# Moving four kinds of transposes of a hybrid decoder block onto one PSUM bank of their own, out of a rotation of four

## The chip, the cores and the metric

The kernel runs on one core of a Trainium2 chip. The metric is the device time of one execution in microseconds, as the median of several runs. Of the kernel before there are three runs, 2709.86, 2710.72 and 2713.3 us, with a median of 2710.72 us.

## What is computed

One layer of a decoder block on 2048 tokens of width 1024, in float32:

```python
h = modulate(rms_norm(x, g_pre), shift, scale)      # adaLN from the conditioning vector c
z = h @ W_in    # attention q|k|v, mLSTM q|k|v|o, mLSTM i|f gates, branch gates A|B
y_A = sliding_window_attention(rope(q), rope(k), v, sinks)   # 8 query heads, 2 kv heads of 64, window 128
y_B = mlstm(conv4_silu(q), conv4_silu(k), v, i, f)           # 4 heads of 128, per-head norm, output gate
x = x + gate * rms_norm((sigmoid(g_A) * (y_A @ W_A) + sigmoid(g_B) * (y_B @ W_B)) @ W_out)
x = x + gate2 * rms_norm(swiglu(modulate(rms_norm(x, .), shift2, scale2)))   # width 2816
```

## The kernel before, in words

**Staging.** The 2048 tokens are done in two superblocks of 1024, sb0 and sb1, each made of two groups b0 and b1 of 512 tokens (four tiles t0 to t3 of 128 rows). A superblock first makes h for b1 (`hprep`, with `one()` at L515 that transposes h, and `hsums` at L552), then the projections of b0 and b1 in the order q and k|v|gates of b0 (`q_kv`), attention in the background, mLSTM values of b0 (`vm`), k|v of b1, q of b1, mLSTM values of b1. Then come the larger projections as a seven-product Strassen-like scheme (`pair_parts`), with the mLSTM chunks in the background, and the output projections. After both superblocks the SwiGLU layer (gate and up, then down) runs, in the same scheme, from about 1250 us on.

**Arithmetic.** A float32 operand is split into a rounded fp32r high part and a low part (`whi` and `wlo` of weights, by ScalarE at L259 and VectorE at L260; `hl` of the pairs at L1356 and L1357), and each product is three matmuls, high·high, high·low, low·high. Scores and the value products of attention run on half of TensorE's rows or columns for each of the two kv heads g0 and g1, so that two matmuls of different heads can lie beside one another.

**PSUM.** There are eight banks. Four carry the tag `acc` (the projections' accumulators) and four the tag `mix`, for all else: the transposes of h (L515), of queries (`q_stream`, L767), of keys (`k_stream`, L794), of the gates (`gates`, L846 and L877), the four score banks of an attention block (L921), its transposed probabilities (L954) and its value products (L966), and in the mLSTM the transposed keys `pk` (L1015), the state updates `pcn` (L1032), the scores `pS` (L1048), the outputs `pn` (L1059) and their transposes `py` (L1086). Later `mix` also holds the FFN's half of the banks (L1398, L1590, L1756).

```python
def mix_tile():
    return ps_mix.tile([P, 512], F32, tag="mix", name=nm("mix"))
```

A pool gives out the banks of one tag in the order in which the program asks for them. The n-th `mix` tile can be written when the (n−4)-th has been read for the last time. On TensorE the first writes of `mix` tiles stand in rising order of their number.

**What sets the order.** The program text interleaves generators by an estimate of elapsed time (`now[0]`); a background stream (a query tile's rotation and transpose, a key tile's, an attention block, an mLSTM chunk) is taken up when its due time has come. What the text asks for first has the smaller tile number. Then, at build time, a scheduler simulates the program with the dependences of its tiles and buffers, and orders the instructions of each engine by it. Each engine then runs its instructions in that fixed order, and waits where an input or a buffer isn't there.

**Other buffers that the steps touch.** The tag `tx` has 9 buffers: an evacuated q tile takes two (`raw` and the rotation's `z`, then the high and low part at L771 and L772, which are written to DRAM as `at_d`), a k|v tile two, an mLSTM value tile one. They come free when the transposes and the DMA out have ended. The probabilities and the mLSTM operands take the tag `tm` (9 buffers). An attention block loads its queries, keys and values from `at_d` into `at`, scores them, makes the softmax (copies L931 and L933, exponentials L946, scaling by GpSimd L950), transposes the probabilities, multiplies by the values (L966) and stores. Two streams of attention blocks run side by side.

Of the kernel before, what the change touches and what calls it, by code (L numbers as in the profile page):

```python
# [19 lines left out]
P = 128  # L20
# [51 lines left out]
def decoder_block(ctx: ExitStack, tc: tile.TileContext, a: dict, out: bass.AP, dbg=None):  # L72
# [24 lines left out]
    def acc_tile():  # L97
        return ps_acc.tile([P, 512], F32, tag="acc", name=nm("acc"))

    def mix_tile():  # L100
        return ps_mix.tile([P, 512], F32, tag="mix", name=nm("mix"))

    def tx(shape, dtype=F32):
        return tpool.tile(shape, dtype, tag="tx", name=nm("tx"), bufs=9)
# [631 lines left out]
    def superblock(sb):  # L736
# [27 lines left out]
        def q_stream(b, t, yz):  # L764
            yield L_ROPE
            y, z = yz
            pt = mix_tile()  # L767
            for j in range(GQ):
                transpose(pt[:, j * P:(j + 1) * P], y[:, j * P:(j + 1) * P])
            hi, lo = z.bitcast(F32R), y.bitcast(F32R)  # L770
            A.activation(hi, pt, AF.Copy, scale=HD ** -0.5)  # L771
            V.scalar_tensor_tensor(lo, pt, HD ** -0.5, hi.bitcast(F32), op0=ALU.mult, op1=ALU.subtract)  # L772
            for i, q in enumerate((hi, lo)):
                nc.sync.dma_start(at_d[b * NT + t][:, i * 512:(i + 1) * 512], q.bitcast(F32))
# [16 lines left out]
        def k_stream(n, yz):  # L791
            yield L_ROPEK
            y, z = yz
            pt = mix_tile()  # L794
            transpose(pt[:, :P], y)
            kk = z[:, P:3 * P].bitcast(F32R).rearrange("p (i k) -> p i k", i=2)
            A.copy(kk[:, 0, :], pt[:, :P])
            V.tensor_tensor(kk[:, 1, :], pt[:, :P], kk[:, 0, :].bitcast(F32), op=ALU.subtract)
            for n_, u in ((n, 1), (n + 1, 0)):
                if n_ < S // P:  # L800
                    nc.sync.dma_start(at_d[n_][:, AT_K:AT_V].rearrange("p (i u k) -> p i u k", i=2, u=2)[:, :, u, :], kk.bitcast(F32))
# [199 lines left out]
        def chunk_state(c):  # L1001
            b, t = b0 + c // NT, c % NT
            negm_d, mp, cl, ex = R["gates", b]
            cs = slice(t * P, (t + 1) * P)
            n_ = b * NT + t
            Cnew = c_tile(n_ + 1)
            km, qm = ld([MH, P]), ld([MH, P])
            nc.sync.dma_start(km, qk_d[b][:, 1, :, cs])
            nb = tm([P, MH, P])
            nc.sync.dma_start(nb, negm_d[:, cs].unsqueeze(0).to_broadcast([P, MH, P]))  # L1010
            nc.sync.dma_start(qm, qk_d[b][:, 0, :, cs])
            vc = vmt[n_ % 2]
            nc.sync.dma_start(vc[:, :, :MD], vm_d[b][:, t, :].rearrange("p (h d) -> p h d", h=MH))
            yield L_LOAD
            pk = mix_tile()  # L1015
            for hh in range(MH):
                transpose(pk[:, hh * P:(hh + 1) * P], km[:, hh, :])
            kw = tm([P, MH, P])
            V.tensor_tensor(kw, pk.rearrange("p (h d) -> p h d", h=MH), ex[:, 0, t, :].unsqueeze(2).to_broadcast([P, MH, P]), op=ALU.mult)
            wd = tm([P, MH, P])  # L1020
            V.tensor_tensor(wd, nb, cneg.unsqueeze(1).to_broadcast([P, MH, P]), op=ALU.add)
            for hh in range(MH):
                A.activation(wd[:, hh, :], wd[:, hh, :], AF.Exp, bias=cl[:, t, 0, hh:hh + 1])
            qs_ = None
            if n_ > 0:
                qs_ = tm([P, MH, P])
                G.tensor_tensor(qs_, nb, mp[:, :, t].unsqueeze(2).to_broadcast([P, MH, P]), op=ALU.add)
                A.activation(qs_, qs_, AF.Exp)
                G.tensor_tensor(qs_, qs_, qm, op=ALU.mult)
            R["w", c] = wd, qs_, km, qm, vc  # L1030
            yield L_KW
            pcn = [mix_tile() for _ in range(2)]  # L1032
            for hh in range(MH):
                mm(pcn[hh // 2][:, (hh % 2) * 129:(hh % 2) * 129 + 129], kw[:, hh, :], vc[:, hh, :], True, True)
            for hh in range(MH):
                o = pcn[hh // 2][:, (hh % 2) * 129:(hh % 2) * 129 + 129]
                if n_ == 0:
                    V.tensor_copy(Cnew[:, hh, :], o)
                else:
                    V.scalar_tensor_tensor(Cnew[:, hh, :], C[n_][:, hh, :], ex[:, 2, t, hh:hh + 1], o, op0=ALU.mult, op1=ALU.add)  # L1040

        def chunk_out(c):
            b, t = b0 + c // NT, c % NT
            negm_d, mp, cl, ex = R["gates", b]
            cs = slice(t * P, (t + 1) * P)
            n_ = b * NT + t
            wd, qs_, km, qm, vc = R["w", c]
            pS = mix_tile()  # L1048
            for hh in range(MH):
                mm(pS[:, hh * P:(hh + 1) * P], km[:, hh, :], qm[:, hh, :], True, True)  # L1050
            V.tensor_tensor(wd, pS.rearrange("p (h t) -> p h t", h=MH), wd, op=ALU.mult)
            yield L_S
            om = tm([P, MH, P])
            nc.sync.dma_start(om, om_d[b][:, :, cs])
            den = small.tile([P, MH], F32, tag="den", name=nm("den"))
            st = small.tile([P, MH, 6], F32, tag="st", name=nm("st"))
            mv = small.tile([P, MH, 2], F32, tag="mv", name=nm("mv"))
            vr = small.tile([P, MH], F32, tag="vr", name=nm("vr"))
            pn = [mix_tile() for _ in range(2)]  # L1059
            for hh in range(MH):  # L1060
                o = pn[hh // 2][:, (hh % 2) * 129:(hh % 2) * 129 + 129]
                if n_ > 0:
                    mm(o, qs_[:, hh, :], C[n_][:, hh, :], True, False)
                mm(o, wd[:, hh, :], vc[:, hh, :], n_ == 0, True)
            for hh in range(MH):
                V.bn_stats(st[:, hh, :], pn[hh // 2][:, (hh % 2) * 129:(hh % 2) * 129 + P])
            for h2 in range(2):
                V.tensor_copy(den[:, 2 * h2:2 * h2 + 2], pn[h2][:, :258].rearrange("p (u w) -> p u w", u=2)[:, :, P])
            for hh in range(MH):
                V.bn_aggr(mv[:, hh, :], st[:, hh, :])  # L1070
            V.scalar_tensor_tensor(den, den, -1.0, den, op0=ALU.mult, op1=ALU.max)
            V.tensor_tensor(den, den, ex[:, 1, t, :], op=ALU.max)
            V.reciprocal(den, den)
            V.tensor_tensor(vr, mv[:, :, 1], den, op=ALU.mult)
            V.tensor_tensor(vr, vr, den, op=ALU.mult)
            V.tensor_scalar(vr, vr, EPS, None, op0=ALU.add)
            cf = small.tile([P, MH], F32, tag="cf", name=nm("cf"))
            G.tensor_tensor(cf, vr, nhalf[:, :MH], op=ALU.pow)
            V.tensor_tensor(cf, cf, den, op=ALU.mult)
            V.scalar_tensor_tensor(vr, mv[:, :, 0], -1.0, cf, op0=ALU.mult, op1=ALU.mult)  # L1080
            ym = tm([P, MH, P])
            for hh in range(MH):
                o = pn[hh // 2][:, (hh % 2) * 129:(hh % 2) * 129 + P]
                A.activation(ym[:, hh, :], o, AF.Identity, scale=cf[:, hh:hh + 1], bias=vr[:, hh:hh + 1])
            yield L_LN
            py = mix_tile()  # L1086
            for hh in range(MH):
                transpose(py[:, hh * P:(hh + 1) * P], ym[:, hh, :])
            V.tensor_tensor(om, py.rearrange("p (h t) -> p h t", h=MH), om, op=ALU.mult)
            yh, yl = tm([P, MH, P], F32R), tm([P, MH, P], F32R)  # L1090
            A.copy(yh, om)
            V.tensor_tensor(yl, om, yh.bitcast(F32), op=ALU.subtract)
            for i, y in enumerate((yh, yl)):
                nc.sync.dma_start(y_d[b][:, 2 + i, :, cs], y.bitcast(F32))
# [283 lines left out]
    def h_combine(b2, rows, quarters, sums):  # L1378
# [14 lines left out]
        for k in range(4):  # L1393
            xk = xn
            v = {}
            for j, (half, i) in enumerate(QUADS):
                kk = k + 4 * half
                ps = mix_tile()  # L1398
                for t in range(4):
                    transpose(ps[:, t * P:(t + 1) * P], xk[j][:, t, :])  # L1400
                q = quarters()
# [64 lines left out]
    def pair_parts(w, c0, done, new, spare, bank):  # L1466
# [4 lines left out]
        def make(i, prep):  # L1471
            B = PROD[i][1]

            def mms(wt):
# [11 lines left out]
                    mm(ps, l[1], r[0], False, kk == 3, True)  # L1486
                    yield
                combine(i, ps, R, new, done)
            return Part(raw, prep, mms, weave=bank is not mix_tile, ahead=4)

        for i, prep in enumerate(a_operands(raw, spare)):
            yield make(i, prep)
# [67 lines left out]
    def gate_up(b2):  # L1560
        late = None
        for p in range(NP):
# [24 lines left out]
                for n, t_ in (("S1", s1_), ("S3", a_["21"]), ("S2", s2_), ("S4", s4_)):  # L1587
                    nc.sync.dma_start(as_d[b2][:, IDX[n], p, :], t_)

            gp, up = (list(pair_parts(w, p * 256, done, unit, unit, mix_tile)) for w, done in ((wg, done_g), (wu, done_u)))  # L1590
            load, sums = down_weights(p)
            if F.get("late") is not None and p == 0:
                def a_step():
# [33 lines left out]
    def down(b2):  # L1627
# [105 lines left out]
        def make(raw, i, p, j):  # L1733
# [16 lines left out]
            def mms(ab):  # L1750
                if p == 0:
                    for t in range(NT):
                        if i == 0:
                            R[t]["X"] = acc_tile()
                        if i not in IN_X:
                            R[t]["Y"] = mix_tile()  # L1756
                if hold:
                    F.setdefault("held", []).append((p, ab))
                    if p == NP - 1:
# [110 lines left out]
```

## Time and profile before

| | |
|---|---|
| median of 3 runs | 2710.72 us (2709.86 to 2713.3) |
| profiled execution, its own time | 2716.59 us |
| its span on the core | 2714.9 us |
| TensorE matmul busy | 2639.2 us, 97% of the span |
| VectorE busy | 1986.2 us, 73% |
| ScalarE busy | 1299.8 us, 48% |
| GpSimd busy | 148.2 us, 5% |

The profiled execution took 5.87 us more than the median. Of TensorE's 75.7 us that aren't busy, 23.5 lie in the first 50 us and 9.1 after 2700 us. In the rows of the trace PE is TensorE, DVE is VectorE, ACT ScalarE, POOL GpSimd. A timeline row gives the start, the time from the start of the first to the end of the last instruction of a group, the engine, line and tiles, and in brackets the idle time before it and who ended it. One value product in float32 is one row of the program and two instructions of the trace.

### The profile page before, as it was taken

To read this page: it belongs to the slowest core of one execution; us is meant where nothing else is said; L and a number is where in the kernel's file an instruction comes from. 1 tells how busy PE (TensorE), PEld (TensorE's weight loads), DVE (VectorE), ACT (ScalarE), POOL (GpSimd) and SP (SyncE) were. 2 spreads that over 40 slices of the span, in tenths; PEclk is the share of its full clock that TensorE was granted. 3 is DMA by queue.
4 is the path that set the end of the run, shared out by engine and by line. 5 is a ranking of instruction groups with operands and counts; after the bars stand their busy time and mean duration, and the time that the engine had idled before them with its cause. 6 is when DMAs were issued, how large, how long until landed. Compare 5 with 4: busy or idle time off the path is not lost.

```text
span 2714.9 us, 35793 instructions
## 1 busy us (share of the span) xinstructions
PE 2639.2 (97%) x12310; PEld 2138.9 (79%) x12310; DVE 1986.2 (73%) x3906; ACT 1299.8 (48%) x2558; POOL 148.2 (5%) x189
## 2 busy tenths in 40 slices
PE   6989999999998999999999999999999999999998
PEld 4867788888885678888887888888877888888886
DVE  7968788778695778876687777776677676766456
ACT  5556544444755564444563443335554333333444
POOL 2010001100101000110000000000000000000000
PEclk8999999999998999999999999999999999999999
DMA  7654355897574544678765564436675232324566
GB/s 249 206 184 157 128 172 179 269 340 248 196 235 147 196 138 138 213 231 291 251 224 198 175 201 152 155 113 213 215 271 188 97 117 86 113 97 144 186 210 217
DMA packets 353639, 511.90 MB, mean 189 GB/s; under 512 B 25120, under 2 KB 213660, under 8 KB 348208
## 3 DMA queue, kind: packets, MB, share of 16 engines
q1 hardware_dynamic: 353456, 509.61, 56.9%
q8 instruction: 97, 1.59, 0.2%
q14 instruction: 86, 0.70, 0.1%
HBM read 357.12 MB, written 144.02 MB: 185 GB/s over the span
## 4 chain that ended last, share of the span: by engine, by line
PE 85%; DVE 7%; DMA 4%; ACT 2%; issue 1%; POOL 0%; SPq 0%; DVEq 0%; ACTq 0%; POOLq 0%
PE acc L204 61%; PE mix L204 22%; PE mix L209 2%; DVE hl L1357 1%; DVE tm L428 1%; DMA raw<-as_d 1%; ACT tm L946 1%; ACT hl L1356 1%; DMA raw<-in_w_in_dram 1%; DMA at_d<-tx 0%; DMA big<-in_x_dram 0%; DVE wlo L260 0%; DMA tx<-in_w_ada_dram 0%; DVE w L1667 0%; DMA at<-at_d 0%
## 5 line engine op out<-in xcount | busy, mean ns | idle before, releaser
L204 PE MATMUL acc<-big,hl 128*128 128x512 f32 x3936 | 940.8, 394 | 4.3 <-ACT tx L827 1.8
L204 PEld LDWEIGHTS acc<-big,hl 128*128 128x128 f32 x3936 | 733.3, 188 | 172.5 <-issue 13.8
L1356 ACT CAST hl<-raw 128x512 fp32r<-128x512 f32 x732 | 440.1, 621 | 493.4 <-PE acc L204 222.2
L1357 DVE TENSOR_TENSOR hl<-raw,hl 128x512 fp32r<-128x512 f32 x732 | 496.3, 694 | 194.8 <-ACT hl L1356 194.0
L204 PE MATMUL acc<-whi,big 128*128 128x512 f32 (+1 forms) x1280 | 379.3, 377 | 10.8 <-ACT big L518 8.4
L204 PEld LDWEIGHTS acc<-whi,big 128*128 128x128 f32 x1280 | 236.2, 192 | 52.4 <-ACT big L518 8.5
L204 PE MATMUL mix<-big,hl 128*128 128x512 f32 x1056 | 263.9, 391 | 1.7 <-ACT hl L1356 1.1
L204 PE MATMUL acc<-wlo,big 128*128 128x512 f32 (+1 forms) x640 | 241.2, 379 | 6.4 <-DVE wlo L260 6.4
L204 PE MATMUL acc<-hl,hl 128*128 128x512 f32 x1008 | 237.4, 393 | 5.1 <-DVE hl L1357 3.4
L204 PEld LDWEIGHTS mix<-big,hl 128*128 128x128 f32 x1056 | 197.9, 188 | 45.9 <-ACT hl L1356 1.9
L204 PEld LDWEIGHTS acc<-hl,hl 128*128 128x128 f32 x1008 | 187.0, 188 | 50.9 <-DVE hl L1357 8.8
L204 PE MATMUL mix<-hl,hl 128*128 128x512 f32 x792 | 182.7, 391 | 1.3 <-DVE hl L1357 0.9
L204 PEld LDWEIGHTS mix<-hl,hl 128*128 128x128 f32 x792 | 147.9, 188 | 35.3 <-DVE hl L1357 3.1
L204 PE MATMUL acc<-big,whi 128*128 128x512 f32 x512 | 157.4, 393 | 0.0
L260 DVE TENSOR_TENSOR wlo<-raw,whi 128x1024 fp32r<-128x1024 f32 (+1 forms) x96 | 109.0, 1137 | 65.5 <-ACT whi L259 59.8
L259 ACT CAST whi<-raw 128x1024 fp32r<-128x1024 f32 (+1 forms) x96 | 94.3, 983 | 123.8 <-PE acc L204 110.4
L204 PEld LDWEIGHTS acc<-wlo,big 128*128 128x128 f32 x640 | 123.7, 193 | 28.3 <-DVE wlo L260 8.6
L475 POOL TENSOR_TENSOR rs<-ms,nhalf 128x1 f32<-128x1 f32 (+1 forms) x56 | 42.6, 772 | 1617.5 <-DVE ms L473 1610.5
L204 PE MATMUL mix<-hcT4h,hl 128*128 128x512 f32 x352 | 117.7, 395 | 0.7 <-ACT hl L1356 0.7
L204 PE MATMUL acc<-hcT2h,hl 128*128 128x512 f32 x352 | 117.6, 394 | 0.0
L204 PEld LDWEIGHTS acc<-big,whi 128*128 128x128 f32 x512 | 95.4, 188 | 19.2
L204 PE MATMUL acc<-big,wlo 128*128 128x512 f32 x256 | 97.7, 393 | 0.0
(330 smaller groups left out, 3491.5 us busy)
## 6 DMA issues: line engine op xcount, KB each, us to landing
raw<-in_w_in_dram SPq DMA_DIRECT2D x48, 1024.0 KB
as_d<-w SPq DMA_DIRECT2D x154, 256.0 KB
raw<-as_d SPq DMA_DIRECT2D x70, 512.0 KB
raw<-in_w_ffn_gate_dram SPq DMA_DIRECT2D x22, 1024.0 KB
raw<-in_w_ffn_up_dram SPq DMA_DIRECT2D x22, 1024.0 KB
raw<-ws_d SPq DMA_DIRECT2D x40, 512.0 KB
y_d<-tm SPq DMA_DIRECT2D x64, 256.0 KB
tx<-in_w_ada_dram SPq DMA_DIRECT2D x64, 256.0 KB
```

The costliest lines, as they stand in the source:

```text
L204: T.matmul(o, lhsT=lhsT, rhs=rhs, start=start, stop=stop, skip_group_check=resumed)
L209: T.transpose(o, i, ident[:k, :k])
L259: A.copy(hv, src)
L260: V.tensor_tensor(lv, src, hv.bitcast(F32), op=ALU.subtract)
L428: V.scalar_tensor_tensor(acc, raw[:, k, :], c_, acc, op0=ALU.mult, op1=ALU.add)
L475: G.tensor_tensor(r[:, :n], ms[:, :n], nhalf[:, :n], op=ALU.pow)
L946: A.activation(sc[g][:, j, :], sc[g][:, j, :], AF.Exp, bias=nm_[:, hd:hd + 1], accum_out=sums[:, hd:hd + 1])
L1356: A.copy(v(hi), src)
L1357: V.tensor_tensor(v(lo), src, v(hi).bitcast(F32), op=ALU.subtract)
```

## The change

`mix` keeps three banks. The fourth gets a tag of its own, `tr`, with one buffer, and is asked for by the four transposes `pt` of queries, `pt` of keys, `pk` and `py`, 16 tiles each over the whole kernel. The transposes of h and of the gates, the attention blocks and the remaining mLSTM tiles ask for `mix` as before. In the FFN a counter sends every fourth request to `tr`, so that there all four banks go round as before.

```diff
+    turn = [0]
+
     def mix_tile():
-        return ps_mix.tile([P, 512], F32, tag="mix", name=nm("mix"))
+        return ps_mix.tile([P, 512], F32, tag="mix", name=nm("mix"), bufs=3)
+
+    def tr_tile():
+        return ps_mix.tile([P, 512], F32, tag="tr", name=nm("tr"), bufs=1)
+
+    def any_tile():
+        turn[0] = (turn[0] + 1) % 4
+        return mix_tile() if turn[0] else tr_tile()
...
         def q_stream(b, t, yz):
-            pt = mix_tile()
+            pt = tr_tile()
...
         def k_stream(n, yz):
-            pt = mix_tile()
+            pt = tr_tile()
...
-            pk = mix_tile()
+            pk = tr_tile()
...
-            py = mix_tile()
+            py = tr_tile()
...
-                ps = mix_tile()
+                ps = any_tile()
...
-            return Part(raw, prep, mms, weave=bank is not mix_tile, ahead=4)
+            return Part(raw, prep, mms, weave=bank is not any_tile, ahead=4)
...
-            gp, up = (list(pair_parts(w, p * 256, done, unit, unit, mix_tile)) for w, done in ((wg, done_g), (wu, done_u)))
+            gp, up = (list(pair_parts(w, p * 256, done, unit, unit, any_tile)) for w, done in ((wg, done_g), (wu, done_u)))
...
-                            R[t]["Y"] = mix_tile()
+                            R[t]["Y"] = any_tile()
```

The text asks for the same tiles in the same order. What the scheduler makes of it differs in the first part of each superblock, and hardly elsewhere. All lines stand 9 further down in the changed program, L204 is L213 there, L209 is L218, L260 is L269.

**TensorE, the attention of b0 and the keys of b1 in sb0.** Of before, in the middle of the third and fourth attention block (`mix252_1614` is the value bank of the fourth, 1797, 1806 and 1815 are transposed keys of b1, `acc301_1973` is an accumulator of the next projection):

```order
L209 MATMUL mix248_1596<-ident_110,tm220_1447 128x128 x4
L204 MATMUL mix252_1614<-tm246_1583,at201_1359 64x512
L209 MATMUL mix278_1797<-ident_110,tx263_1704 128x128
L209 MATMUL mix279_1806<-ident_110,tx265_1726 128x128
L204 MATMUL mix252_1614<-tm249_1601,at201_1359 64x512
L204 MATMUL mix252_1614<-tm247_1585,at201_1359 64x512
L204 MATMUL mix252_1614<-tm250_1603,at201_1359 64x512
L209 MATMUL mix280_1815<-ident_110,tx267_1746 128x128
L204 MATMUL acc301_1973<-whi287_1906,big85_665 128x512
```

Of the change, at the second of those key tiles (210 and 211 are score banks of the third block, 221 one of the fourth):

```order
L213 MATMUL mix210_1388<-at194_1328 128x256 x4
L213 MATMUL mix211_1389<-at194_1328 128x256 x4
L213 MATMUL mix210_1388<-at194_1328 128x256
L213 MATMUL mix211_1389<-at194_1328 128x256
L213 MATMUL mix221_1448<-at201_1359 128x256 x6
L218 MATMUL tr279_1806<-ident_110,tx265_1726 128x128
L213 MATMUL acc274_1788<-whi282_1844,big90_689 128x512
L213 MATMUL acc274_1788<-wlo283_1845,big90_689 128x512
L213 MATMUL acc274_1788<-whi282_1844,big91_690 128x512
```

The key tiles stood behind the fourth block's value bank, with no accumulating matmul between the pieces; now they stand ahead of it, at the fourth block's first score bank, with accumulating matmuls behind them, and the fourth block's scores of one head (`mix221` x6) stand apart from those of the other (`mix222`, 22 rows further down).

**VectorE, weights of the values of b0 in sb0.** Of before, around the low part of the third-next weight tile (`wlo157_1111`; `tx...` at L757 to L761, L810 and L811 are rotations and value differences of the k|v tiles, L535 to L537 sums of h, L835 the begin of the gates' chain):

```order
L521 TENSOR_TENSOR big91_690<-big69_539,big90_689 128x512
L813 TENSOR_TENSOR gt_197<-tx126_984,b_if_100 128x4
L760 TENSOR_TENSOR tx122_944<-tx122_944,tx123_946 128x2x32
L761 TENSOR_TENSOR tx122_944<-tx122_944,tx123_946 128x2x32
L260 TENSOR_TENSOR wlo157_1111<-raw115_868,whi156_1110 128x1024
L535 TENSOR_TENSOR big68_538<-big69_539,big68_538 128x512
L536 TENSOR_TENSOR big69_539<-big69_539,big10_204 128x512
L759 TENSOR_TENSOR tx126_984<-tx126_984,cos56_479 128x128
```

Of the change, ahead of the same weight tile (L561 is L552 of before, `hsums`; L844 to L853 are L835 to L844, the gates' chain; L781 is L772):

```order
L781 TENSOR_SCALAR tx95_720<-tr110_814,tx96_722 128x512
L561 TENSOR_TENSOR big238_1550<-big238_1550,big260_1686 128x512 x4
L766 TENSOR_TENSOR tx127_986<-tx126_984,sin55_478 128x2x32
...
L844 TENSOR_SCALAR sp140_1046<-gt_197 128x16
...
L852 TENSOR_TENSOR sp143_1049<-sp143_1049,sp142_1048 128x16
L853 TENSOR_SCALAR gt_197<-gt_197,sp143_1049 128x4x4
L269 TENSOR_TENSOR wlo157_1111<-raw115_868,whi156_1110 128x1024
L269 TENSOR_TENSOR wlo182_1279<-raw115_868,whi181_1278 128x1024
```

The low part `wlo157_1111` stood ahead of the last sums of h, of `hsums` and of the gates' chain; now it stands behind all of these. Ahead of it are 13 further instructions of 512 columns (one L535, two L536, two L537, eight `hsums`) and 19 small ones.

## The prediction

> **What bounds the kernel now.** The page's first part and its chain come first.
>
> ```profile
> PE 2639.2 (97%) x12310; PEld 2138.9 (79%) x12310; DVE 1986.2 (73%) x3906; ACT 1299.8 (48%) x2558; POOL 148.2 (5%) x189
> ...
> PE 85%; DVE 7%; DMA 4%; ACT 2%; issue 1%; POOL 0%; SPq 0%; DVEq 0%; ACTq 0%; POOLq 0%
> ```
>
> TensorE is busy 97% of the span and carries 85% of the chain that ends last. So a PSUM bank can win only where TensorE is not at work or is at work slowly. The question is where that is, and the busy time by stretch answers it.
>
> ```profile
> 163.50:184.50 21.00, 14.14 (x67) 6.65 (x66) 11.06 (x34) 13.07 (x49) 4.68 (x5) 0.84 0.26 82
> ...
> 836.40:866.40 30.00, 20.58 (x94) 10.30 (x92) 13.81 (x40) 14.56 (x52) 4.67 (x5) 0.72 0.39 121
> ```
>
> ```profile
> 400.00:545.00 145.00, 145.00 (x775) 124.07 (x774) 112.80 (x286) 68.04 (x139) 24.18 (x21) 1.00 0.74 230
> 1100.00:1245.00 145.00, 145.00 (x786) 124.36 (x785) 113.77 (x295) 66.94 (x133) 26.27 (x22) 1.00 0.75 240
> ```
>
> After the length of the stretch stand the busy times of PE, PEld, DVE, ACT and POOL, then the granted clock. In 400–545 and 1100–1245 us, where the mLSTM runs beside the large projections, TensorE is busy without a gap at full clock: nothing can be won there. In 163.5–184.5 and 836.4–866.4 us it is idle for 6.86 and 9.42 us, 16.3 us in all, at clocks of 0.84 and 0.72. The timeline of TensorE shows what stands there, in sb0:
>
> ```profile
> 163.51 0.97 PE L204 MATMUL mix<-at 64*128 64x256 f32 x6
> 167.22 1.70 PE L204 MATMUL mix<-at 64*128 64x256 f32 x24 [2.75 <-DMA at<-at_d]
> 170.71 1.39 PE L209 MATMUL mix<-ident,tm 128*128 128x128 f32 x8 [1.79 <-DVE tm L933]
> 172.07 4.09 PE L204 MATMUL mix<-tm,at 128*64 128x512 f32 x8
> 177.59 0.65 PE L209 MATMUL mix<-ident,tm 128*128 128x128 f32 x4 [1.42 <-POOL tm L950]
> 179.03 1.04 PE L209 MATMUL mix<-ident,tm 128*128 128x128 f32 x4 [0.79 <-POOL tm L950]
> ...
> 184.47 0.48 PE L204 MATMUL acc<-whi,big 128*128 128x512 f32 x1
> ```
>
> and in sb1:
>
> ```profile
> 841.08 2.74 PE L204 MATMUL mix<-at 64*128 64x256 f32 x24 [2.43 <-DMA at<-at_d]
> 845.10 2.93 PE L204 MATMUL mix<-at 64*128 64x256 f32 x24 [1.28 <-DVE tm L933]
> 852.09 2.24 PE L209 MATMUL mix<-ident,tm 128*128 128x128 f32 x8 [4.06 <-DVE tm L933]
> 854.26 4.37 PE L204 MATMUL mix<-tm,at 128*64 128x512 f32 x8
> ...
> 866.40 0.48 PE L204 MATMUL acc<-whi,big 128*128 128x512 f32 x1
> ```
>
> Two attention blocks run through here alone: load, scores, softmax, transposes, value products, and no `acc` matmul from 163.51 to 184.47 us, nor up to 866.40 us in sb1. The reason is in the order: the key transposes of b1 (1797, 1806, 1815) stand in the rotation behind the fourth block's value bank (1614). Until they run, their `tx` buffers stay taken, and the projection that needs new ones has nothing more to issue. Call each such stretch a clump.
>
> **The change, part by part.**
>
> *Clumps, the gain.* With keys on `tr` the order puts 19 or 20 `acc` matmuls between two key transposes and 10 to 27 between pieces of attention. Both clumps go. What is won is their length less the work in them at its usual pace. The paces:
>
> ```profile
> 246.13 1.07 PE L204 MATMUL mix<-tm,at 128*64 128x512 f32 x2
> 247.13 0.74 PE L204 MATMUL acc<-big,hl 128*128 128x512 f32 x2
> ```
>
> ```profile
> 255.44 1.08 PE L204 MATMUL mix<-tm,at 128*64 128x512 f32 x4
> 256.45 0.74 PE L204 MATMUL acc<-big,hl 128*128 128x512 f32 x2
> ```
>
> ```profile
> 220.21 0.98 PE L204 MATMUL mix<-at 64*128 64x256 f32 x12
> 221.11 0.47 PE L209 MATMUL mix<-ident,tm 68*128 68x68 f32 x4
> 221.51 0.97 PE L204 MATMUL mix<-at 64*128 64x256 f32 x6
> 222.41 0.50 PE L204 MATMUL acc<-big,hl 128*128 128x512 f32 x1
> ```
>
> From start to next start, four gate transposes take 0.40 us, so some 0.1 each. Twelve scores that alternate between the heads take 0.90, 0.075 each. A value product is two trace instructions, and a pair of them, one for each head, takes 1.0 us. In sb0 30 scores (2.3 to 2.7 us), 16 probability and 3 key transposes (1.9) and four pairs of value products, one of them split (4 to 5) make about 9.4 of 20.96 us: 11.5 are won. In sb1 the stretch from 836.4 to 866.4 holds one more half-block, about 13 of 30: 17 are won. Together **−28 us**. The least is the idle time alone, −16; as the most I keep −28, since the work in them stays.
>
> *Split pairs, a cost.* A block asks for four score banks, and there are three now. The same rows show what that does: six scores of one head alone take 0.90 us, as long as twelve that alternate. A value product alone takes 1.00, a pair of two heads 1.01. In the new order runs of six scores alone go from 10 to 18, and lone value products from 20 to 31, since other work comes between. Counting the runs of all attention matmuls in each order (0.15 us for a score of one head, 1.0 for a value product, the heads side by side where adjacent) gives 81.7 us before and 94.6 now: **+13 us** of TensorE time. At the other end, if softmax waits are anyway what is filled, it is 0.
>
> *Switches.* Breaking up the runs makes 23 more changes between `acc` and `mix` matmuls.
>
> ```profile
> 155.85 1.07 PE L204 MATMUL mix<-tm,at 128*64 128x512 f32 x2
> 156.85 0.50 PE L204 MATMUL acc<-whi,big 128*128 128x512 f32 x1
> 157.19 0.39 PE L204 MATMUL acc<-wlo,big 128*128 128x512 f32 x1
> 157.42 0.63 PE L204 MATMUL acc<-whi,big 128*128 128x512 f32 x2
> ```
>
> The first `acc` matmul after a piece takes 0.34 us to the next start, the second 0.23: 0.11 more, 23 times, **+2.5 us**; between 0 and 5.
>
> *VectorE's queue, a cost.* Queries share one bank, so h's transposes go ahead of them. With these VectorE's work on h (L521, L534 to L537), the `hsums` (L552) and the gates' chain (L835 to L844) moves ahead of the weights' low parts (L260), on which TensorE's next projection waits. In sb0 VectorE has no time for that:
>
> ```profile
> 70.00:80.00 10.00, 7.46 (x58) 6.56 (x58) 10.00 (x23) 8.47 (x14) 0.00 (x0) 1.00 0.14 52
> 80.00:90.00 10.00, 10.00 (x72) 9.34 (x72) 10.00 (x26) 7.13 (x12) 0.00 (x0) 1.00 0.96 295
> 90.00:100.00 10.00, 10.00 (x46) 8.26 (x46) 10.00 (x32) 5.21 (x9) 0.00 (x0) 1.00 0.60 177
> ```
>
> ```profile
> 96.76 1.22 DVE L260 TENSOR_TENSOR wlo<-raw,whi 128x1024 fp32r<-128x1024 f32 x1
> 97.89 0.68 DVE L535 TENSOR_TENSOR big<-big,big 128x512 f32<-128x512 f32 x1
> ```
>
> ```profile
> 98.36 0.47 PE L204 MATMUL acc<-wlo,big 128*128 128x512 f32 x1
> ```
>
> VectorE is busy all of 70 to 100 us. `wlo157_1111` is the row at 96.76; it ends at 97.98 (the next starts at 97.89 already), and TensorE takes it at 98.36: some 0.4 to 0.7 us of slack. Thirteen more 512-column instructions stand ahead of it now, each some 0.60 us (0.68 of the row, less the overlap of about 0.08 with which 97.89 follows a 1.22 us row of 96.76): 7.8 us; the 19 small ones add about 2.5, so 10.3. TensorE's first use has moved by 0.4 us only. So TensorE waits 9.6 us in all, of which about 3.0 already for `wlo119_911`, with five more 512-column instructions ahead of it. Behind the waiting matmul stands everything, TensorE being in order; DVE's surplus later has nobody waiting. Sb1 repeats it: 7.4 us more ahead of `wlo_7384` and 9.0 ahead of `wlo_7581`, where TensorE waits for such tiles already:
>
> ```profile
> 745.73 0.39 PE L204 MATMUL acc<-wlo,big 128*128 128x264 f32 x1 [0.92 <-DVE wlo L260]
> ```
>
> I take **+9.6 and +9.0 us**. At the other end, 0, if the h work comes late by other waits and the weights wait for their loads anyway; but the busy 30 us speak against that.
>
> *mLSTM.* `pk` and `py`, some 9 us apart, share a bank; each is cleared by one VectorE instruction:
>
> ```profile
> L1019 DVE TENSOR_TENSOR tm<-mix,ex 128x512 f32<-128x512 f32 x8 | 5.4, 681 | 0.0
> ```
>
> Covered by the projections' matmuls, which make TensorE 100% busy there: 0. Without cover, 16 chunks by two such evacuations, +22 us. The FFN keeps four banks and its order: 0.
>
> *Sum:* −28 + 13 + 2.5 + 18.6 = **+6 us** on the profiled execution of 2716.6. This stood 5.9 over the median, so the sum goes onto 2710.7: **2717 us**.
>
> *Where the skill speaks.* The clump at 841 us had a granted clock of 0.72 although four banks turned. The Trainium skill, "TensorE: Matmul & The Clock Gate", section "A second HAM failure mode: psum-queue depth-cycling", says that small idle times between groups of matmuls, when PSUM banks are cycled, make the clock step down and up again, so that throughput falls with no long gap. The trace agrees that idling stretches run slow; by this rule a single bank with short waits would lose clock as well, and the sum would stand above 2717. The skill's "Perfetto Trace Analysis", section "Matmuls", has independent groups rotate through different banks so that an evacuation overlaps the next group. That speaks against one bank for 64 tiles; no run here shows yet what one bank costs.
>
> **The rivals.**
>
> *The stalls are absorbed.* The clumps go, the splits cost 13 and the switches 2.5, but VectorE catches up: −28 + 15.5 = −12.5, **2698 us**. For it: the scheduler that ordered VectorE saw these instructions as ready and the weights as not urgent; ScalarE, which makes `whi` first, isn't full (5.21 of 10 in 90–100). Against it: VectorE's 30 us at 10.00. If the split pairs cost nothing either, −26, 2685.
>
> *One bank chains the queries* (ends slower). Query tiles queue for one bank, each cleared by ScalarE (L771) and VectorE (L772), and the latter stands behind h work. So the last query tiles give their `tx` buffers back late, and TensorE's next evacuation, in order, waits. Two such tiles per superblock, each with one L772 behind a full VectorE and a load like the `at<-at_d` wait of 2.75 us:
>
> ```profile
> 82.11 0.69 DVE L772 SCALAR_TENSOR_TENSOR tx<-mix,tx 128x512 fp32r<-128x512 f32 x1
> ```
>
> 4 × (0.69 + 2.75) = +14 over the sum, +20, **2731 us**. It decides as soon as the query transposes lie more than a few us behind their evacuations; in before all four were done at 84.5 us.
>
> *The mLSTM waits after all:* +22 over the sum, 2739 us. Against it: no idle time there now.
>
> *Nothing happens.* TensorE being 97% busy, moves of small pieces cancel, or the clumps come back elsewhere: 2711 us.
>
> **How the numbers follow.** My sum has a chance of 0.43, with its own range of 2710 to 2724 (terms a few us off each way). Absorbed stalls 0.23, chained queries 0.24, the mLSTM 0.04, nothing 0.06. A measurement of this kernel can tell 0.2%, 5.4 us, from no change. Slower by more (above 2716.1): 0.27 of my sum's 0.43, with 0.24 and 0.04: 0.55. Within: 0.14 of the sum, the 0.06 of nothing and 0.01 of absorbed stalls: 0.21. Faster: 0.22 of absorbed stalls and 0.02 of the sum: 0.24. The range runs from 2694, a few us under the absorbed case, to 2735, above the chained one; 0.1 is left out at each end.
>
> **What would show it.** Right for the clumps: no stretch of 20 us without `acc` matmuls near 165 and 840 us, and the clock there near 1. Right for the splits: TensorE's `mix<-at` and `mix<-tm,at` groups longer by about 13 us in sum, in more pieces. Right for VectorE: waits of several us of `acc` matmuls on `wlo L260` near 87–110 and 750–790 us. Wrong: if such waits are below 2 us, the time falls to 2698 or less; if waits on `tx` or on L772 stand there, the chain rival is it; if gaps open in 400–545 us, the mLSTM is.

## The result, and the profile after

| | before | changed |
|---|---|---|
| median (4 runs each) | 2711.38 us (2709.86 to 2713.3) | 2723.8 us (2720.99 to 2725.67) |
| ratio, 95% interval | | 1.0044 (1.0029 to 1.0058) |
| profiled execution | 2716.59 us | 2725.67 us |
| TensorE busy | 2639.2 us | 2651.2 us |

The change makes the kernel slower by 0.44%, some 12 us; +6 had been forecast, 2717 in a range of 2694 to 2735. The two profiled executions lie 9.1 us apart.

First the busy time by stretch of the changed kernel, in the columns of before (length, PE, PEld, DVE, ACT, POOL, granted clock, DMA's share and GB/s):

```profile
57.00:100.00 43.00, 34.69 (x208) 29.72 (x207) 36.74 (x84) 27.45 (x53) 5.09 (x6) 0.96 0.44 141
100.00:163.50 63.50, 59.30 (x308) 44.59 (x308) 42.01 (x148) 35.45 (x94) 4.17 (x4) 0.95 0.58 182
163.50:210.00 46.50, 46.50 (x227) 33.65 (x227) 32.31 (x71) 26.20 (x71) 4.83 (x5) 1.00 0.67 221
760.00:836.00 76.00, 65.43 (x368) 54.50 (x368) 61.98 (x192) 38.88 (x94) 2.09 (x2) 0.91 0.66 219
836.00:870.00 34.00, 34.00 (x159) 22.86 (x159) 22.12 (x56) 13.68 (x30) 2.55 (x2) 1.00 0.58 172
```

and the same stretches of before:

```profile
57.00:100.00 43.00, 40.46 (x245) 35.45 (x245) 38.42 (x94) 31.79 (x60) 5.20 (x6) 1.00 0.47 147
100.00:163.50 63.50, 61.45 (x346) 49.12 (x345) 46.85 (x143) 35.96 (x93) 4.70 (x4) 0.97 0.67 213
163.50:210.00 46.50, 39.61 (x194) 27.19 (x194) 35.59 (x83) 27.22 (x75) 4.68 (x5) 0.93 0.63 214
760.00:836.00 76.00, 72.71 (x394) 59.40 (x394) 62.14 (x192) 43.94 (x103) 4.53 (x4) 0.98 0.68 223
836.00:870.00 34.00, 24.58 (x115) 13.67 (x113) 17.47 (x49) 16.56 (x57) 4.67 (x5) 0.75 0.45 137
```

Rows 3 and 5 are the clumps: they are full now, at a clock of 1.00, where before had 39.61 and 24.58 us of work at 0.93 and 0.75. Rows 1, 2 and 4 are the starts of the superblocks: there TensorE lost 5.77, 2.15 and 7.28 us of busy time, and the clock fell. So the gain came as forecast, and more was lost ahead of it.

How much, can be had from the count of TensorE's instructions: the time at which the changed kernel has done as many as before had done. Counted by the starts of the matmuls in the two traces, it lags by 14.8 us at 100 us, by 16.8 at 150, by 9.0 at 200; by 10.7 at 700, by 24.2 at 780, by 23.6 at 840 and by 6.7 at 950; by 8.1 at 1600 and by 9.1 at 2700. (The order differs, so a few us of this are small instructions against large ones, inside a start; behind it, the numbers compare.) The starts cost 16.8 and 13.5 us, the clumps gave back 7.8 and 16.9.

What TensorE waits for most in the first start, 57 to 163.5 us, of the changed kernel (in all, times, longest), and what ScalarE waits for there:

```profile
PE acc L213 <- ACT tx L815: 6.5, 3, 2.9
PE mix L218 <- ACT big L529: 2.0, 3, 1.2
PE tr L218 <- DVE tx L781: 1.4, 1, 1.4
PE acc L213 <- DVE wlo L269: 1.0, 1, 1.0
```

```profile
ACT tx L780 <- PE tr L218: 9.9, 2, 8.9
```

and in the second (700 to 836 us), TensorE again:

```profile
PE tr L218 <- DVE tx L781: 6.9, 2, 5.0
PE acc L213 <- DVE wlo L269: 3.1, 2, 1.8
PE acc L213 <- ACT tx L815: 1.6, 2, 1.1
```

For the low parts `wlo` the kernel before waited, in the same two stretches:

```profile
PE acc L204 <- DVE wlo L260: 2.6, 2, 2.1
```

```profile
PE acc L204 <- DVE wlo L260: 3.2, 5, 1.3
```

They had been forecast to cost 18.6 us more; TensorE waits 4.1 us for them, where it had waited 5.8. All its waits in the two starts went from 10.0 to 24.3 us, and most of these are for other things: 8.3 us for the query bank's second evacuation (L781, L772 of before) and 8.1 for the copy of a k|v accumulator to SBUF (L815, L806 of before). The rows of VectorE and ScalarE between 84 and 98 us show how these hang together:

```profile
91.79 0.68 DVE L781 SCALAR_TENSOR_TENSOR tx<-tr,tx 128x512 fp32r<-128x512 f32 x1
97.83 0.68 DVE L781 SCALAR_TENSOR_TENSOR tx<-tr,tx 128x512 fp32r<-128x512 f32 x1
```

```profile
85.93 0.59 ACT L780 ACTIVATE tx<-tr 128x512 fp32r<-128x512 f32 x1
87.65 0.38 ACT L815 COPY tx<-acc 128x264 f32<-128x264 f32 x1 [1.13 <-DMA at_d<-tx]
96.96 0.60 ACT L780 ACTIVATE tx<-tr 128x512 fp32r<-128x512 f32 x1 [8.93 <-PE tr L218]
```

ScalarE has read the second query tile at 86.5 us, but VectorE, which has h's sums ahead, clears the bank at 92.5 only. The third tile's transposes come behind that in TensorE's order, at 96.3 us, and ScalarE, in order too, idles 8.93 us until they are there. (TensorE doesn't wait for the bank at that point: accumulating matmuls stand ahead of these transposes, and the bank is free 3.8 us before they start. So the delay is in part the order that the scheduler made, and only in part a wait.) The k|v copies (L815) stand in ScalarE's queue behind the query tiles; the row at 87.65 also shows one waiting for a `tx` buffer that a DMA to `at_d` must free.

### The profile page after: what moved, and what is told of

Same layout as the page of the kernel before. It is cut to its first block, busy times and chain, and to the rows that moved or that the text cites. A ratio compares the mean times of both kernels' runs of the same rounds, so it can differ in the third digit from the quotient of the medians.

```text
span 2724.0 us, 35756 instructions
## 1 busy us (share of the span) xinstructions
PE 2651.2 (97%) x12310; PEld 2140.5 (79%) x12310; DVE 1983.6 (73%) x3906; ACT 1300.1 (48%) x2558; POOL 148.0 (5%) x189
## 4 chain that ended last, share of the span: by engine, by line
PE 81%; DVE 9%; DMA 5%; ACT 3%; issue 1%; POOL 0%; SPq 0%; DVEq 0%; POOLq 0%; ACTq 0%
PE acc L213 57%; PE mix L213 18%; PE tr L213 4%; DVE hl L1366 1%; DMA raw<-as_d 1%; DVE wlo L269 1%; DVE tm L437 1%; ACT hl L1365 1%; PE mix L218 1%; PE tr L218 1%; DVE big L1366 1%; DMA tm<-negm_d 0%; ACT tm L955 0%; DMA big<-big 0%; DMA big<-g_d 0%
## 5 line engine op out<-in xcount | busy, mean ns | idle before, releaser
L213 PE MATMUL acc<-big,hl 128*128 128x512 f32 x3936 | 938.9, 392 | 2.0 <-ACT hl L1365 0.9
L213 PEld LDWEIGHTS acc<-big,hl 128*128 128x128 f32 x3936 | 731.6, 188 | 169.5 <-issue 10.6
L213 PE MATMUL acc<-whi,big 128*128 128x512 f32 (+1 forms) x1280 | 386.0, 381 | 15.6 <-ACT tx L815 8.1
L213 PEld LDWEIGHTS acc<-whi,big 128*128 128x128 f32 x1280 | 237.3, 193 | 66.7 <-ACT tx L815 10.2
L213 PE MATMUL acc<-wlo,big 128*128 128x512 f32 (+1 forms) x640 | 243.3, 381 | 4.2 <-DVE wlo L269 4.0
L213 PE MATMUL acc<-hl,hl 128*128 128x512 f32 x1008 | 236.9, 393 | 5.0 <-DVE hl L1366 3.3
L213 PEld LDWEIGHTS acc<-hl,hl 128*128 128x128 f32 x1008 | 187.1, 188 | 50.1 <-DVE hl L1366 8.5
L213 PE MATMUL mix<-big,hl 128*128 128x512 f32 x792 | 197.9, 390 | 1.1 <-DVE hl L1366 0.7
L213 PEld LDWEIGHTS mix<-big,hl 128*128 128x128 f32 x792 | 148.3, 188 | 33.7 <-DVE hl L1366 1.1
L213 PE MATMUL mix<-hl,hl 128*128 128x512 f32 x594 | 158.4, 391 | 2.5 <-ACT hl L1365 1.5
L213 PE MATMUL acc<-big,whi 128*128 128x512 f32 x512 | 157.8, 393 | 0.0
L269 DVE TENSOR_TENSOR wlo<-raw,whi 128x1024 fp32r<-128x1024 f32 (+1 forms) x96 | 109.3, 1141 | 63.3 <-ACT whi L268 60.0
L213 PEld LDWEIGHTS acc<-wlo,big 128*128 128x128 f32 x640 | 123.9, 194 | 30.7 <-DVE wlo L269 7.2
L213 PEld LDWEIGHTS mix<-hl,hl 128*128 128x128 f32 x594 | 110.7, 188 | 29.5 <-DVE hl L1366 3.4
L213 PE MATMUL acc<-hcT2h,hl 128*128 128x512 f32 x352 | 117.5, 394 | 0.0
L213 PEld LDWEIGHTS acc<-big,whi 128*128 128x128 f32 x512 | 95.3, 188 | 19.2
L213 PE MATMUL acc<-big,wlo 128*128 128x512 f32 x256 | 97.9, 393 | 0.0
L213 PE MATMUL mix<-hcT4h,hl 128*128 128x512 f32 x264 | 88.2, 394 | 0.7 <-ACT hl L1365 0.7
```

The lines of the kernel that those rows point to most:

```text
L213: T.matmul(o, lhsT=lhsT, rhs=rhs, start=start, stop=stop, skip_group_check=resumed)
L269: V.tensor_tensor(lv, src, hv.bitcast(F32), op=ALU.subtract)
```

## The experiments

Each was timed in several rounds beside the kernel before on the same chip. All edits are to the changed kernel where nothing else is said. Each edit lets the scheduler order the whole program anew, so a ratio is that of the edit with its order. "On `tr`" is the bank of its own, "in the rotation" the three banks `mix`.

| run | on `tr` | median, before | ratio (95%) |
|---|---|---|---|
| changed | q, k, pk, py | 2723.8, 2711.4 | 1.0044 (1.0029–1.0058) |
| e1 | k, pk, py | 2705.5, 2711.8 | 0.9978 (0.9969–0.9987) |
| e2 | none | 2719.9, 2711.8 | 1.0023 (1.0014–1.0032) |
| e3 | q | 2738.7, 2711.8 | 1.0100 (1.0086–1.0114) |
| e4 | q, k | 2728.0, 2711.8 | 1.0058 (1.0044–1.0071) |
| e5 | q of b1, k, pk, py | 2694.1, 2709.8 | 0.9942 (0.9930–0.9955) |
| e6 | q of b0, k, pk, py | 2724.7, 2709.8 | 1.0054 (1.0041–1.0066) |
| e7 | as changed, h's low parts on GpSimd | 2725.3, 2709.8 | 1.0054 (1.0040–1.0068) |
| e8 | as e1, and every 4th h tile | 2699.7, 2709.8 | 0.9962 (0.9950–0.9975) |
| e9 | as changed, bank cleared by one copy | 2712.1, 2709.4 | 1.0010 (1.0001–1.0019) |
| e10 | as e5, and 2 of b0's 4 q tiles | 2702.8, 2709.4 | 0.9975 (0.9966–0.9984) |
| e11 | as e5, and every 4th h tile | 2688.4, 2709.4 | 0.9923 (0.9910–0.9935) |
| e12 | as e11, bank cleared by one copy | 2706.6, 2710.2 | 0.9985 (0.9976–0.9994) |

**Queries back in the rotation (e1).**

```diff
         def q_stream(b, t, yz):
-            pt = tr_tile()
+            pt = mix_tile()
```

> Edit: the query transposes go back to the rotation of three; keys, pk and py stay on the bank of their own. Theory (the loss of the change sits in the query tiles that queue for one bank at the start of each superblock, some 15 us in sb0 and 11 us in sb1; the gain is the two clumps, 7.4 us in sb0 and 14 us in sb1): the clumps stay away, the start is as before, about 2711 - 21 + 5 for split pairs = 2695 us. Rival (three banks for scores and values, or VectorE's queue, cost it): no better than the change, 2718 to 2726 us.

2705.5 us, 6 faster than before and 18 faster than the change: the theory's side, though 10 us above its number. The loss of the change hangs on the queries.

**No transposes on the bank (e2), queries alone (e3), and pk and py back (e4).** The edit of each is the same exchange at other places:

```diff
-            pt = tr_tile()     # q_stream in e2; k_stream in e2 and e3
+            pt = mix_tile()
-            pk = tr_tile()     # and py, in e2, e3 and e4
+            pk = mix_tile()
```

> Edit: all four kinds of transposes back to the rotation of three; the fourth bank is used in the FFN only. Theory: three banks by themselves cost little; the clumps stay, the start is as before, 2708 to 2718 us. Rival (three score banks split the pairs and hold the mLSTM up): over 2722 us.

> Edit: only the query transposes on the bank of their own; keys, pk and py back to the rotation of three. Theory: the start loses its 15 and 11 us and the clumps stay: 2711 + 26 + 0 to 8 for split pairs = 2737 to 2745 us. Rival (the queries' bank costs nothing, keys or mLSTM operands do): 2711 to 2715 us.

> Edit: pk and py back to the rotation of three; queries and keys stay on the bank of their own. Theory: nothing waits for them, TensorE being busy without a gap in the mLSTM's stretches: 2721 to 2726 us as the change. Rival (pk and py on one bank wait for each other): faster than the change by up to 16 x 0.7 = 11 us, 2712 us.

Taking a bank out of the rotation alone costs 8 us (e2), more than the theory and less than the rival said. In the profiled executions e2 lags behind before by 2.0 us at 150 us, 4.8 at 400, 9.0 at 700, 5.1 at 1100 and 5.3 at 2700: what is lost from 400 to 700 us, where the mLSTM has seven tiles per chunk through three banks, is mostly back by 1100, so the counts don't place the loss there. Queries alone on top (e3) make +27, as forecast, 19 more than e2. Keys on top of the queries (e3 to e4) take 11 off. With `pk` and `py` on the bank (e4 to the changed kernel) it is 3.8 us less, with intervals that overlap; e4 itself lies 2 us above its range. The changed kernel isn't slower than e4, so no cost of `pk` and `py` waiting for one another shows. The two clumps of before answer to the keys: in e3 they are still there,

```profile
163.50:190.00 26.50, 22.21 (x109) 13.15 (x105) 14.40 (x40) 15.49 (x53) 4.68 (x5) 0.87 0.40 121
...
860.00:885.00 25.00, 19.42 (x88) 11.67 (x86) 9.83 (x29) 13.27 (x48) 4.15 (x4) 0.80 0.29 89
```

and in e4 they are gone:

```profile
163.50:190.00 26.50, 26.50 (x143) 20.10 (x143) 21.00 (x56) 17.00 (x55) 4.30 (x4) 1.00 0.51 154
860.00:885.00 25.00, 25.00 (x140) 20.34 (x138) 21.82 (x54) 18.47 (x57) 5.10 (x4) 1.00 0.64 213
```

**Which query tiles (e5, e6).**

```diff
-            pt = tr_tile()
+            pt = tr_tile() if b % 2 else mix_tile()     # e5; e6 the other way round
```

> Edit: of the query tiles only those of the second group b1 of each superblock go to the bank of their own (with keys, pk and py); those of b0 go back to the rotation. Theory (the loss is where the query tiles of b0 meet the transposes of h and VectorE's work on h, at the start of each superblock): as without any query tile there, 2703 to 2709 us. Rival (each query tile on one bank costs the same): half-way, about 2715 us.

> Edit: the mirror of the run before, only the query tiles of b0 on the bank of their own (with keys, pk and py), those of b1 in the rotation. Theory: all of the loss, 2720 to 2726 us. Rival (each tile the same): about 2715 us.

The tiles of b0 carry the loss: e6 is at +15 us. Those of b1 are a gain: e5 is some 9 us below e1 (15.6 under its before against 6.3), and below its expected range. (With b0's tiles on the bank as well, the same step, e6 to the changed kernel, is worth only 2.5 us, with intervals that overlap.) The same stretch of e1 and of e5 shows where:

```profile
185.00:210.00 25.00, 21.44 (x87) 12.11 (x86) 18.70 (x35) 14.99 (x40) 3.01 (x3) 0.86 0.38 122
```

```profile
185.00:210.00 25.00, 25.00 (x113) 17.18 (x113) 21.22 (x41) 18.57 (x47) 3.05 (x3) 1.00 0.71 220
```

In e1 (upper row) a new, shorter clump stands at 185 to 210 us: b1's query tiles wait in the rotation behind the attention banks, as the keys did before. In e5 they don't, and the stretch is full.

**What holds the bank (e7, e9).** One edit takes work from VectorE's queue, the other takes VectorE out of the clearing:

```diff
-            (G if first else V).tensor_tensor(lo, v, hi.bitcast(F32), op=ALU.subtract)
+            G.tensor_tensor(lo, v, hi.bitcast(F32), op=ALU.subtract)     # e7
```

```diff
-            A.activation(hi, pt, AF.Copy, scale=HD ** -0.5)     # e9
-            V.scalar_tensor_tensor(lo, pt, HD ** -0.5, hi.bitcast(F32), op0=ALU.mult, op1=ALU.subtract)
+            A.activation(y, pt, AF.Copy, scale=HD ** -0.5)
+            A.copy(hi, y)
+            V.tensor_tensor(lo, y, hi.bitcast(F32), op=ALU.subtract)
```

> Edit to the change: the low parts of h (eight 512-column subtractions for each group of 512 tokens, L530 of the change) go from VectorE to GpSimd for all groups, where before only the first group's were there; 24 instructions leave VectorE. Theory A (the query tiles' bank is cleared late because L781 stands in VectorE's full queue): the start of each superblock gains 8 x 0.6 = 4.8 us of VectorE's time, the waits on L781 and L815 shrink, 2712 to 2718 us. Theory B (the one bank's own chain of transposes, two evacuations and a write, whatever VectorE's queue): 2721 to 2727 us.

> Edit to the change: ScalarE copies the query bank to SBUF at once, and the high and low part are then made from that copy (16 more ScalarE instructions of some 0.6 us), so that the one bank is free after one ScalarE instruction and no longer after VectorE's L781. Theory A (the loss at the start of each superblock is that the one bank is cleared through VectorE's queue, in sb0 from the transposes at 85 us to L781's end at 92.4 us): most of the start's loss goes, 2700 to 2712 us. Theory B (it is the order in which h's transposes and VectorE's h work go ahead, or the buffers tx, whatever clears the bank): 2720 to 2728 us.

e7 gained nothing, so theory A failed there as it was put. It isn't a clean test: on GpSimd these instructions take longer, and from 57 to 163.5 us the waits for `wlo` rose from 1.0 to 6.2 us and those for L781 from 1.4 to 4.4, while those for L815 fell from 6.5 to 1.0.

```profile
L530 POOL TENSOR_TENSOR big<-big,big 128x512 fp32r<-128x512 f32 x32 | 53.5, 1686 | 68.3 <-ACT big L529 65.3 <-DMA x1n<-tm 2.7
```

```profile
PE acc L213 <- DVE wlo L269: 6.2, 3, 4.8
PE tr L218 <- DVE tx L781: 4.4, 2, 3.0
```

They take 1.69 us on average where VectorE's rows had 0.68. e9 is the more direct test, since the bank itself is cleared sooner: 9.8 us faster than the change, each against its before, at the edge of what theory A expected. The transposes of b0's four query tiles, in the kernel before:

```profile
74.92 0.60 PE L209 MATMUL mix<-ident,tx 128*128 128x128 f32 x4
75.79 0.60 PE L209 MATMUL mix<-ident,tx 128*128 128x128 f32 x4
76.83 0.63 PE L209 MATMUL mix<-ident,tx 128*128 128x128 f32 x4 [0.44 <-DVE tx L761]
78.03 0.66 PE L209 MATMUL mix<-ident,tx 128*128 128x128 f32 x4 [0.57 <-ACT big L520]
```

in the changed kernel:

```profile
75.12 0.60 PE L218 MATMUL tr<-ident,tx 128*128 128x128 f32 x4
84.90 0.60 PE L218 MATMUL tr<-ident,tx 128*128 128x128 f32 x4
96.32 0.60 PE L218 MATMUL tr<-ident,tx 128*128 128x128 f32 x4
104.25 0.61 PE L218 MATMUL tr<-ident,tx 128*128 128x128 f32 x4
```

and in e9:

```profile
74.85 0.60 PE L218 MATMUL tr<-ident,tx 128*128 128x128 f32 x4
79.30 0.65 PE L218 MATMUL tr<-ident,tx 128*128 128x128 f32 x4
85.10 0.60 PE L218 MATMUL tr<-ident,tx 128*128 128x128 f32 x4
87.49 0.65 PE L218 MATMUL tr<-ident,tx 128*128 128x128 f32 x4 [1.46 <-ACT tx L780]
```

They start within 3.1 us before, within 29.1 in the changed kernel and within 12.6 in e9. Of what is left in e9 (18 us over e5) the trace shows one part: ScalarE's copy of a k|v accumulator, L816 there, waits for `tx`:

```profile
ACT tx L816 <- DMA at_d<-tx: 7.8, 1, 7.8
```

**A dose of it (e10), and the gains together (e11).** In e10 the condition of e5 is `b % 2 or t < 2`. e11 is e5 with h going round all four banks:

```diff
         def one(k):
-            ps = mix_tile()
+            ps = any_tile()
```

> Edit to the kernel with queries back in the rotation: the transposes of h go round all four banks, every fourth to the bank of the keys. If what three banks cost lies at h's transposes, this gives it back: 2698 to 2702 us. If not, 2703 to 2709 us, or more where a key's transposes now wait for h's evacuation.

> Edit to the run with only the query tiles of b1 on the bank of their own: of b0's four tiles the first two go there too, the last two stay in the rotation. Theory (each further tile in the chain costs its wait; one wait of three remains of some 21 to 30 us): 2694 + 7 to 10 = 2701 to 2704 us. Rival (one tile put off is enough to turn the order round): 2710 us or more.

> Edit: both gains together, query tiles of b0 in the rotation and of b1 on the bank of their own (with keys, pk and py), and h's transposes going round all four banks. If they add up, 2694 - 6 = 2686 to 2690 us; if the h transposes only stood in for what the b1 tiles give, 2692 to 2697 us.

e8 gives back 4 us of what three banks cost, against e1 in ratio; e10 lies at 9 us above e5, as expected for one wait in the chain; and in e11 the gains add up, as far as the intervals tell. At 2688.4 us, 21 us under before, e11 beats both kernels. Its starts and its clump of sb1:

```profile
57.00:100.00 43.00, 40.78 (x242) 36.11 (x241) 38.63 (x94) 31.06 (x59) 4.84 (x6) 0.96 0.46 147
...
836.00:870.00 34.00, 34.00 (x176) 25.61 (x176) 24.78 (x52) 24.92 (x69) 4.16 (x4) 1.00 0.67 222
```

TensorE does as much up to 100 us as before, and the second clump stays full.

**A control (e12).** The copy of e9, put into e11.

> Edit: the copy that clears the query bank at once, put into the fastest kernel so far (query tiles of b0 in the rotation, of b1 on the bank of their own, h round all four banks), as a control. Theory (the copy helped the change because it shortened the one bank's chain for b0's tiles): here no such chain waits, so no gain, 2685 to 2693 us. Rival (the copy helps by itself, by taking VectorE off PSUM): some 10 us less, 2677 to 2681 us.

Each against its before, it is 17 us slower than e11, slower than either expectation. So the copy is no gain by itself, and that e9 gained by what the copy does to b0's chain is the likely reading, not a shown one. Why it costs so much here stays open; the waits of TensorE for `wlo` and for ScalarE's copies are longer in it (3.8 and 4.6 us from 700 to 960 us; in e11 1.2 for `wlo`, and none of 0.4 us or more for the copies, though 3.2 for `whi`, which e12 doesn't wait for).

## Why the prediction was right, and where it wasn't

The terms can be held against the two profiled executions, whose spans differ by 9.1 us. The time from each matmul's start to the next one's falls into idle time, time that a granted clock below full adds, and the rest, the work at full clock.

- **Clumps, −28:** right in cause and nearly in size. From 163.5 to 210 and from 836 to 960 us, idle time and the clock's share went from 33.6 to 1.6 us, −32.0. (The lag falls by less, 24.7, since it also counts work that takes longer in these stretches, split pairs among it.) e3 and e4 show that the keys' place in the rotation was the cause.
- **Split pairs, +13, and switches, +2.5:** right in size. At full clock the scores and value products take 79.2 us before and 90.9 in the changed kernel, +11.7; all other work grew by 6.0 us, and the switches' share of that wasn't separated. The busy time of the two groups, of before and of the change, hides this:

```profile
L204 PE MATMUL mix<-tm,at 128*64 128x512 f32 x124 | 51.7, 695 | 0.0
L204 PE MATMUL mix<-at 64*128 64x256 f32 x360 | 37.9, 308 | 7.3 <-DMA at<-at_d 5.2 <-DVE tm L933 1.3 <-DVE cl L883 0.8
```

```profile
L213 PE MATMUL mix<-tm,at 128*64 128x512 f32 x124 | 52.0, 616 | 0.0
L213 PE MATMUL mix<-at 64*128 64x256 f32 x360 | 42.6, 293 | 1.9 <-DMA at<-at_d 1.1 <-ACT tm L940 0.8
```

  Busy time went from 89.6 to 94.6 us, only +5.0, as before's part was stretched by the clumps' low clock. The reason given, three score banks instead of four, doesn't hold by itself: with three banks the same work takes 78.8 us in e2, 82.1 in e5 and 82.8 in e11. It is the order that splits the pairs, and b0's queries on the one bank, by which the changed kernel differs from e5, are part of what made that order. And e2, which splits no more pairs than before, still costs 8 us, so three banks have a price of their own that the sum did not hold.
- **VectorE's queue, +18.6:** the step that failed, though its size fits. From 57 to 163.5 and from 700 to 836 us idle time and the clock's share grew from 13.5 to 34.1 us, +20.6, but the wait is another: TensorE waited 4.1 us for `wlo`, less than the 5.8 of before, and longer for the query bank's second evacuation and for the k|v copy behind it. The prediction took the tile's place in VectorE's queue for the time at which TensorE would miss it; TensorE was held up sooner, by L815 and L781, and came to those matmuls late. The rival *one bank chains the queries* named these waits. e5, e6 and e10 show that the loss hangs on b0's query tiles on the one bank, and e9 points to the late clearing of that bank. The rival put +14 us on top of the VectorE term; in truth it stands in its place.
- **mLSTM, 0:** right; `pk` and `py` on one bank cost nothing that shows (e4).
- **The sum, +6, measured +12 (+9.1 between the profiled executions):** it came out near by luck, because the wrong term had about the size of the true one.
- The sentence on the Trainium skill's "TensorE: Matmul & The Clock Gate", section "A second HAM failure mode: psum-queue depth-cycling", agrees with the starts: with more waits, of up to 5.0 us, they had clocks of 0.96, 0.95 and 0.91, where before had 1.00, 0.97 and 0.98. Over the whole execution the clock didn't fall (0.990 before, 0.992 in the changed kernel), since the clumps' low clock went away, so it is not the clock that put the time above 2717.

What stays open: how the remaining 18 us of e9 over e5 divide between the `tx` buffers and the order itself, and how much of the loss of b0's tiles is waiting and how much is attention cut into more pieces. A tenth `tx` buffer wasn't tried.

## What to carry to other kernels

A buffer of its own for a class of tiles helped those that in the common rotation stood behind a slow consumer (keys and later queries behind attention's banks), and hurt those that came in a row, four at once, with a clearing that passed through two engines' queues. Split the class by where its tiles come, not by what they are: the same query transposes cost 21 us in one place (e6 against e1, each against its before) and gained 9 in another (e5 against e1). And when an instruction is found later in a queue, follow which wait comes first in the in-order engine that would miss it, before that wait is priced.

## What the runs showed that was not expected

Taking one of four banks out of the rotation and using it for nothing in that phase (e2) cost 8 us (1.0023, 1.0014 to 1.0032), though TensorE idles for only 1.4 of the 300 us from 400 to 700 us, where the mLSTM goes through three banks. In the profiled executions, 5.6 us apart in span, the idle time is nearly the same in all (75.7 us before, 76.4 in e2); what differs is the granted clock, 0.988 against 0.990 over the whole span, which is worth some 5 us (an estimate, 0.002 of the span). Why the clock is lower with three banks wasn't found out.
